# Four narrow modulation products per tile instead of two wide ones, issued together on TensorE

## The chip, the cores and the metric

The kernel runs on one core of one Trainium2 chip. The metric is the device time of one execution in microseconds (us), the median of several runs.

## What is computed

The reference chains two small diffusion-transformer parts over 256 tokens of 1024 features, in float32. Every sublayer is modulated by a condition vector `c`: the vector goes through SiLU and is multiplied by a matrix of modulation weights, which gives rows of 1024 values for shift, scale and gate. Cut to what matters here:

```python
cond = silu(c)                                   # 1 x 1024
for i in range(2):                               # first block: two layers
    shift, scale, gate = split(cond @ ada_w[i] + ada_b[i], 3)
    h = rms_norm(x, norm_g[i]) * (1 + scale) + shift
    x = x + gate * mixer(h)                      # attention with its projections
c_act = silu(c_2)                                # second block
shift1, scale1, gate1, shift2, scale2, gate2 = split(c_act @ w_ada + b_ada, 6)
h = rms_norm(x, norm1_g) * (1 + scale1) + shift1
x = x + gate1 * (attention(h) @ w_out)
h2 = rms_norm(x, norm2_g) * (1 + scale2) + shift2
x = x + gate2 * peer(h2)                         # routing to 16384 small experts
out = rms_norm(x, final_g)
```

The twelve rows of 1024 modulation values are computed as six groups `g` of 2048 columns, each the product of a 1024-long condition and a 1024 x 2048 matrix.

## The kernel before, in words

The program runs through layer 0 (to about 280 us), layer 1 (to about 410 us), the second block's attention (to about 560 us) and the expert stage (to the end). Most matrix products are made from split operands: a float32 tile is split into a high part (ScalarE, line 186) and the rest (VectorE, line 211), and three matmuls (lines 239 to 241) are summed for each product. Weights come in tiles of 512 KB through SyncE's queue (SP): `load_raw` at line 229 for projections, lines 362 and 390 for modulation.

A modulation group is computed by `ada(g)`. The condition, one column for each slice `k` of 128 features, is repeated to 32 columns and is the stationary operand (128 x 32), so a product fills 32 of TensorE's 128 columns, one of four column groups; `tile_position=(0, 32 * q)` names the group. For each of eight slices `k` and each half `h` of the 2048 columns, line 390 loads a tile `adaw` of 128 x 1024 values, and lines 391 to 394 multiply it as two products of 512 columns: half 0 goes to column groups 0 and 1, half 1 to groups 2 and 3. All add up in one PSUM tile `psa` of 128 x 512, whose partitions 32q to 32q + 31 hold the 512 values of quarter `q`. There are 16 tiles and 32 products in a group. Three buffers `adaw` are shared by all tiles. After the last product, line 400 adds the bias row, and for shift and scale `ada_cols` (line 406) turns rows into columns. Operands are float32 without a split; a product then shows in the trace as two weight loads and two matmul records.

Group 0 is needed first and has a function of its own, `ada_first` (line 365), before 50 us. Groups 1 to 5 are the steps `a1` to `a5` in the hand-written order of each layer. There `@-4` shifts a step by four times 50 places to the front:

```python
ORDER = {'0': '... s010 z0 a1@-4 q1 ... v01@-4 s100 a2@-4 z2 ... o O a3@-1',
 '1': ...
 '2': '... sa1 oa1 vb tb sb0@5 a4 ob0@1 sb1 a5 o ob1 O@5'}
```

The order of the steps gives priorities only. When the program is built, a planner with a model of the durations walks through it and puts each engine's instructions into a fixed order: of those whose operands are there by its model, the one with the first priority. At run time every engine and the SP queue keep that order, and wait at an instruction whose operands are late. So the planner places the products of a tile wherever TensorE has a place by its model; the products of one tile need not stand together.

Other lines that the prediction names: 517 (the transposed and normalised input), 631 (transposes of queries and keys), 701 and 706 (transposes of probabilities and their product with the values), 725 and 1117 (attention scores), 820 (the compression product of layer 0: float32 products of 256 columns in two column groups of 64), 898 (transpose of compressed probabilities), 985 (gate logits), 1206 (values of the second block).

Of the kernel before, what the change touches and what calls it, by code (L numbers as in the profile page):

```python
# [21 lines left out]
NK = 8  # L22
# [84 lines left out]
def _consts():  # L107
    c = np.zeros((128, _CW), np.float32)
    p = np.arange(128)

    def put(name, v):
        o, w = _CST[name]
        c[:, o:o + w] = v

    put("ident", np.eye(128))
    put("mask2", np.concatenate([np.zeros((128, 128)), np.where(p[None] > p[:, None], NEG, 0.0)], 1))
    cm = np.full((128, 2, 16), NEG)
    for tt in range(2):
        for n in range(15):
            cm[:, tt, n] = np.where(16 * n + 31 <= tt * 128 + p, 0.0, NEG)  # L120
    put("cmask", cm.reshape(128, 32))
    put("rowok", np.stack([p >= 31, p >= -1], 1))
    put("rmask", p[:, None] // 32 == np.arange(4)[None])
    sel = np.zeros((128, 2, 64))
    for par in range(2):
        sel[2 * np.arange(64) + par, par, np.arange(64)] = 1
    put("sel", sel.reshape(128, 128))
    put("sel4", p[:, None] == 32 * np.arange(4)[None])
    sr = np.zeros((128, 4, 128))
    for j in range(4):  # L130
        sr[32 * j, j, :] = 1
    put("selrow", sr.reshape(128, 512))
    put("iota", np.broadcast_to(p[None], (128, 128)))
    inv = np.array([0x3f800000, 0x3e4693af, 0x3d1a08c8, 0x3beef74e, 0x3ab95d22, 0x398fc8f8,
                    0x385f10c4, 0x372d07a7], np.uint32).view(np.float32)
    put("invf", np.broadcast_to(inv[None], (128, 8)))
    cc = np.arange(64)
    st = np.clip(cc - 8, 0, 48)
    win = (cc[None] >= st[:, None]) & (cc[None] < st[:, None] + 16)
    put("namask", np.tile(np.where(win, 0.0, NEG), (2, 1)))  # L140
    put("ones", 1.0)
    t5 = np.zeros((128, 1024), np.float32)
    for i in range(512):
        rel = min(i - 255, 255)
        t5[_bucket(rel), i] = 1.0
        t5[:, 512 + i] = 0.0 if abs(rel) <= 128 else NEG
    return c, t5


class Net:  # L150
# [230 lines left out]

    def ada(self, g):

        nc, a = self.nc, self.a
        ci = 0 if g < 3 else 8
        ps = self.pp.tile([128, 512], F32, name="psa", tag="psa", bufs=1)
        for k in range(NK):
            for h in range(2):
                raw = self.cp.tile([128, 1024], F32, name="adaw", tag="adaw", bufs=CFG["adaw"])
                nc.sync.dma_start(raw, a["adaw"][g, k, :, h * 1024:(h + 1) * 1024])  # L390
                for j in range(2):
                    q = 2 * h + j
                    nc.tensor.matmul(ps[32 * q:32 * q + 32], self.cond[:, ci + k, :], raw[:, j * 512:(j + 1) * 512],  # L393
                                     start=(k == 0), stop=(k == NK - 1), tile_position=(0, 32 * q))
        gate = g in (1, 4)
        r = self.cp.tile([128, 512], F32, name="adar", tag=f"adar{gate}")
        for q in range(4):
            nc.sync.dma_start(r[32 * q:32 * q + 32], bass.AP(tensor=a["adab"].tensor, offset=(g * 4 + q) * 512,
                                                            ap=[[0, 32], [1, 512]]))
        nc.vector.tensor_tensor(r, ps, r, op=OP.add)  # L400
        if gate:
            self.gr = r
        else:
            self.mods[g] = self.ada_cols(r, ps, (2, 3, 5).index(g) + 1)
# [1189 lines left out]
def _arrays(i):  # L1594
    f = {k: np.ascontiguousarray(np.asarray(v)) for k, v in i.items()}
    o = {}
    o["x"] = f["x"].reshape(S, D)
    cst, t5 = _consts()
    o["cst"], o["t5c"] = cst, t5
    o["cc"] = np.concatenate([f["c"].reshape(8, 128).T, f["c_2"].reshape(8, 128).T], 1)  # L1600
    pos = f["positions"].reshape(S)
    o["pos"] = pos.reshape(2, 128).T
    o["posc"] = np.tile(pos[np.minimum(16 * np.arange(16) + 31, 255)], 4).reshape(64, 1)
    cols = lambda g: g.reshape(8, 128).T
    o["ng"] = np.stack([cols(f["norm_g"][0]), cols(f["norm_g"][1]), cols(f["norm1_g_2"][0]), cols(f["norm2_g_2"][0])], 1)
    o["rows"] = np.concatenate([f["nsa_gate_b"][0], f["nsa_q_norm"][0], f["nsa_k_norm"][0].reshape(-1),
                                f["moba_q_norm"][0], f["moba_k_norm"][0], f["sink_a_2"][0]])
    W, B = f["ada_w"], f["ada_b"]
    W2, B2 = f["w_ada_2"][0], f["b_ada_2"][0]
    split = np.concatenate([np.arange(512) + o for o in (0, 1024, 512, 1536)])  # L1610
    parts = [(W[0][:, split], B[0][split]),
             (np.concatenate([W[0][:, 2048:], W[1][:, 2048:]], 1), np.concatenate([B[0][2048:], B[1][2048:]])),
             (W[1][:, 0:2048], B[1][0:2048]),
             (W2[:, 0:2048], B2[0:2048]),
             (np.concatenate([W2[:, 2048:3072], W2[:, 5120:6144]], 1), np.concatenate([B2[2048:3072], B2[5120:6144]])),
             (W2[:, 3072:5120], B2[3072:5120])]
    o["adaw"] = np.stack([p[0].reshape(8, 128, 2048) for p in parts])
    o["adab"] = np.stack([p[1].reshape(4, 512) for p in parts])

    kt = lambda w, n=512: w.reshape(4, 2, 128, -1, n).transpose(3, 0, 2, 1, 4).reshape(-1, 4, 128, 2 * n)  # L1620

    zt = lambda w: w.reshape(2, 4, 128, -1, 256).transpose(3, 0, 2, 1, 4).reshape(-1, 2, 128, 1024)
    zp = np.concatenate([np.concatenate([np.arange(64) + 64 * (4 * (2 * p + a) + r) for a in range(2)])
                         for p in range(2) for r in range(4)])
    w = f["nsa_w_in"][0]
    o["w0"] = kt(np.concatenate([w[:, 1024:1536], w[:, 1536:1792], w[:, 2048:2304], w[:, 1792:2048], w[:, 2304:2560],
                                 w[:, 0:1024]], 1))
    g = np.zeros((1024, 128), np.float32)
    g[:, :48] = w[:, 2560:2608]
    o["w0g"] = g.reshape(8, 128, 128).transpose(1, 0, 2).reshape(128, 1024)  # L1630
    o["gb"] = f["nsa_gate_b"][0].reshape(48, 1)
    o["w0z"] = zt(w[:, 2608:3632][:, zp])
    o["w0o"] = kt(f["nsa_w_out"][0][zp])
    o["pe"] = f["nsa_cmp_pe"][0].reshape(2, 16, 128).transpose(2, 0, 1)
    o["cw1"] = f["nsa_cmp_w1"][0].reshape(2, 4, 4, 128, 256).transpose(0, 1, 3, 2, 4).reshape(2, 4, 128, 1024)
    o["cb1"] = f["nsa_cmp_b1"][0]
    o["cw2"] = f["nsa_cmp_w2"][0].reshape(2, 2, 128, 64).transpose(2, 0, 1, 3)
    w = f["moba_w_in"][0]
    o["w1"] = kt(np.concatenate([w[:, 1024:1536], w[:, 0:1024]], 1))
    o["w1z"] = zt(w[:, 1536:2560][:, zp])  # L1640
    o["w1o"] = kt(f["moba_w_out"][0][zp])
    w = f["w_in_2"][0]
    o["w2s"] = kt(w[:, 512:768], 256)[0]
    o["w2"] = kt(np.concatenate([w[:, 0:512], w[:, 768:2304]], 1))
    za = np.concatenate([np.concatenate([np.arange(64) + 64 * (4 * a + r) for a in range(2)]) for r in range(4)])
    w = f["w_out_2"][0]
    o["w2o"] = kt(np.concatenate([w[0:512][za], w[512:]], 0))
    o["on"] = np.concatenate([f["out_norm_a_2"][0][za].reshape(4, 128).T, f["out_norm_b_2"][0].reshape(4, 128).T], 1)
    o["t5t"] = f["t5_table_2"]
    o["rpb"] = f["rpb_b_2"].reshape(8, 15, 31)  # L1650
    o["wq"] = zt(f["w_query_2"][0])
    o["keys"] = f["sub_keys_2"][0].reshape(16, 128, 128).transpose(2, 0, 1)
    o["u"] = f["u_experts_2"][0].reshape(128, 128, 8, 128).transpose(0, 3, 2, 1).reshape(128, 128, 1024)
    o["v"] = f["v_experts_2"][0].reshape(128, 128, 1024)
    o["fg"] = f["final_g_2"]
    return {k: np.ascontiguousarray(v) for k, v in o.items()}
# [16 lines left out]
```

## Time and profile before

| | us |
|---|---|
| median of 3 runs | 1414.01 (1412.24 to 1414.22) |
| the profiled execution | 1413.74 |
| its span in the trace | 1412.0 |
| TensorE busy in the span | 1366.8 (97%) |
| VectorE busy | 1023.2 (72%) |
| ScalarE busy | 821.9 (58%) |
| matmuls of line 393, busy | 81.3 |

Times in the trace count from the start of the span. A row of the timeline is a run of like records of an engine, with its start, its length and the number of records; the end of a matmul is modelled and reaches into the next one, so a cost is read from one start to the next start. A float32 product of line 393 or 820 has two records. In the windows, "busy" is the union of an engine's records in that stretch and the number in brackets counts them. "PEld" is TensorE's loading of the stationary operand. In the list of waits, "SPq" is the queue in which SyncE issues the loads.

### The profile page before, as it was taken

Reading aid. Unit: us, or ns where it says so; the run is one execution under the profiler, and the core shown is the slowest. Engines: PE = TensorE matmul, PEld = TensorE weight load, DVE = VectorE, ACT = ScalarE, POOL = GpSimd, SP = SyncE. Lnnn points to the kernel's source line nnn. Section 1 sums busy time; section 2 is a strip of 40 time slices with the busy share of each in tenths; the row PEclk is TensorE's granted clock in tenths of the full one; section 3 lists DMA queues with packets and bytes.
Section 4 is the critical chain, followed back from the end, with each engine's and each line's share of the span. In section 5 each row is a group of like instructions: output and inputs, shape, how many; then the busy total and the mean of one; then the engine's idle time right before and its main releaser. Section 6 shows DMA issues by size and latency. Waiting matters only on the chain.

```text
span 1412.0 us, 24444 instructions
## 1 busy us (share of the span) xinstructions
PE 1366.8 (97%) x8522; PEld 1120.8 (79%) x8522; DVE 1023.2 (72%) x2636; ACT 821.9 (58%) x1887; POOL 21.9 (2%) x27
## 2 busy tenths in 40 slices
PE   6999999999989998999999999999999999999997
PEld 2566666477767755999999999999998888888885
DVE  3585756388665656799999968888866666677777
ACT  2353656357646654555555568888865555555554
POOL 0000000000001100000000000000000000000001
PEclk9999999999999999999999999999999999999999
DMA  8577564553486766455555555554456665677773
GB/s 309 199 272 273 197 203 138 199 186 101 138 313 199 216 225 223 135 182 179 179 179 179 181 188 193 165 164 162 165 194 227 194 194 194 194 227 239 245 242 114
DMA packets 94875, 279.15 MB, mean 198 GB/s; under 512 B 11112, under 2 KB 30320, under 8 KB 94624
## 3 DMA queue, kind: packets, MB, share of 16 engines
q1 hardware_dynamic: 94752, 277.59, 59.6%
q8 instruction: 67, 1.10, 0.3%
q14 instruction: 56, 0.46, 0.1%
HBM read 267.80 MB, written 13.94 MB: 200 GB/s over the span
## 4 chain that ended last, share of the span: by engine, by line
PE 90%; DVE 4%; DMA 4%; ACT 1%; issue 1%; SPq 0%; ACTq 0%; DVEq 0%
PE ps L240 18%; PE ps L239 18%; PE ps L241 18%; PE acc L240 5%; PE acc L239 5%; PE acc L241 5%; PE psa L393 5%; PE ps L1493 4%; PE ps L706 2%; DMA raw<-in_w1o 1%; PE ps L725 1%; PE ps L701 1%; PE psa L365 1%; DMA adaw<-in_adaw 1%; DVE lo L211 1%; PE ps L631 1%
## 5 line engine op out<-in xcount | busy, mean ns | idle before, releaser
L186 ACT CAST hi<-raw 128x512 fp32r<-128x512 f32 (+1 forms) x700 | 429.4, 618 | 349.9 <-PE ps L240 147.1
L211 DVE TENSOR_TENSOR lo<-raw,hi 128x512 fp32r<-128x512 f32 (+1 forms) x700 | 479.8, 688 | 179.7 <-ACT hi L186 162.8
L239 PE MATMUL ps<-hh,hi 128*128 128x256 f32 x1160 | 333.0, 287 | 1.3 <-DVE hh L187 1.3
L240 PE MATMUL ps<-hl,hi 128*128 128x256 f32 x1160 | 328.3, 283 | 1.1 <-DVE hl L211 1.1
L241 PE MATMUL ps<-hh,lo 128*128 128x256 f32 x1160 | 328.4, 283 | 0.0
L239 PEld LDWEIGHTS ps<-hh,hi 128*128 128x128 f32 x1160 | 222.6, 192 | 1.5 <-issue 1.5
L240 PEld LDWEIGHTS ps<-hl,hi 128*128 128x128 f32 x1160 | 222.4, 192 | 1.3 <-DVE hl L211 1.3
L241 PEld LDWEIGHTS ps<-hh,lo 128*128 128x128 f32 x1160 | 222.2, 192 | 0.0
L239 PE MATMUL ps<-hi,Ah 128*128 128x512 f32 x508 | 198.1, 390 | 0.0
L240 PE MATMUL ps<-lo,Ah 128*128 128x512 f32 x508 | 197.7, 389 | 0.0
L241 PE MATMUL ps<-hi,Al 128*128 128x512 f32 x508 | 197.6, 389 | 0.0
L239 PEld LDWEIGHTS ps<-hi,Ah 128*128 128x128 f32 x508 | 95.4, 188 | 20.1 <-issue 0.2
L241 PEld LDWEIGHTS ps<-hi,Al 128*128 128x128 f32 x508 | 95.4, 188 | 19.9
L240 PEld LDWEIGHTS ps<-lo,Ah 128*128 128x128 f32 x508 | 95.4, 188 | 19.9 <-DVE lo L211 0.2
L1492 ACT ACTIVATE og<-o,gT 128x128 f32<-128x128 bf16 x256 | 87.2, 394 | 4.1 <-DVE o L1490 0.3
L393 PE MATMUL psa<-adaw,cond 128*32 128x512 f32 x320 | 81.3, 610 | 3.1 <-DMA adaw<-in_adaw 3.1
L240 PE MATMUL acc<-lo,hh 128*128 128x512 f32 (+1 forms) x176 | 70.7, 402 | 2.4 <-DVE lo L211 2.4
L239 PE MATMUL acc<-hi,hh 128*128 128x512 f32 (+1 forms) x176 | 69.6, 401 | 2.6 <-DVE hh L187 1.4
L241 PE MATMUL acc<-hi,hl 128*128 128x512 f32 (+1 forms) x176 | 69.9, 398 | 0.0
L1493 PE MATMUL ps<-og,o 128*128 128x128 f32 x512 | 65.2, 275 | 0.1
L1493 PEld LDWEIGHTS ps<-og,o 128*128 128x128 f32 x512 | 61.4, 192 | 0.3 <-ACT og L1492 0.3
L733 ACT ACTIVATE P<-P,nm 128x128 f32<-128x128 f32 (+1 forms) x96 | 42.6, 446 | 13.5 <-DVE nm L730 13.4
(397 smaller groups left out, 1929.8 us busy)
## 6 DMA issues: line engine op xcount, KB each, us to landing
raw<-in_u SPq DMA_DIRECT2D x128, 512.0 KB, 3.6
raw<-in_v SPq DMA_DIRECT2D x128, 512.0 KB, 4.3
adaw<-in_adaw SPq DMA_DIRECT2D x86, 512.0 KB, 4.9
raw<-in_w SPq DMA_DIRECT2D x48, 512.0 KB, 4.3
raw<-in_wq SPq DMA_DIRECT2D x16, 512.0 KB, 3.4
zd<-ge SPq DMA_DIRECT2D x56, 128.0 KB, 1.7
ge<-zd SPq DMA_DIRECT2D x56, 128.0 KB, 3.6
raw<-in_adaw SPq DMA_DIRECT2D x10, 512.0 KB, 7.0
```

The lines of the kernel that those rows point to most:

```text
L186: return self.nc.scalar.copy(out, in_)
L211: return self.nc.vector.tensor_tensor(lo, src, hi.bitcast(F32), op=OP.subtract)
L239: mm(out, a[0][asl], b[0][bsl], start=first, stop=False, **kw)
L240: mm(out, a[0][asl], b[1][bsl], start=False, stop=False, **kw)
L241: mm(out, a[1][asl], b[0][bsl], start=False, stop=last, **kw)
L365: nc.tensor.matmul(ps[32 * q:32 * q + 32], self.cond[:, k, :], raw[:, j * 512:(j + 1) * 512], start=(k == 0), stop=(k == NK - 1), tile_pos ...
L393: nc.tensor.matmul(ps[32 * q:32 * q + 32], self.cond[:, ci + k, :], raw[:, j * 512:(j + 1) * 512], start=(k == 0), stop=(k == NK - 1), til ...
L631: nc.tensor.transpose(pr[:P, i * 128:i * 128 + 128], s.rearrange("p a d -> p (a d)") if P == 128 else s, self.identr)
L706: nc.tensor.matmul(o[64 * a:64 * a + 64], v[br][kb][:, 2 * pair + a, :], pts[a], start=first, stop=False, tile_position=(0, 64 * a), skip_ ...
L733: nc.scalar.activation(Pb, Pb, AF.Exp, scale=-1.0, bias=nm[:, r, br:br + 1], accum_out=sums[:, r, br:br + 1])
L1492: nc.scalar.activation(og[:, j], o1[:, j], AF.Copy, scale=gT[:, t0 + j:t0 + j + 1])
L1493: nc.tensor.matmul(ps[:, j * 128:j * 128 + 128], o2[:, j], og[:, j], start=(j == 0), stop=(j == 3), skip_group_check=True)
```

## The change

A tile `adaw` now holds 256 columns of each of the four quarters. It is multiplied as four products of 256 columns, one for each column group; half `h` fills columns 256h to 256h + 255 of `psa`. The three products after the first get a priority that is 2000 places ahead, and an edge for the planner that puts them behind the first. The start flag stands at the first half of the first slice alone, the stop flag at the second half of the last. The array `adaw` is rearranged to fit for groups 1 to 5; group 0 and `ada_first` stay as they were.

```diff
@@ def ada(self, g)
             for h in range(2):
                 raw = self.cp.tile([128, 1024], F32, name="adaw", tag="adaw", bufs=CFG["adaw"])
                 nc.sync.dma_start(raw, a["adaw"][g, k, :, h * 1024:(h + 1) * 1024])
-                for j in range(2):
-                    q = 2 * h + j
-                    nc.tensor.matmul(ps[32 * q:32 * q + 32], self.cond[:, ci + k, :], raw[:, j * 512:(j + 1) * 512],
-                                     start=(k == 0), stop=(k == NK - 1), tile_position=(0, 32 * q))
+                first = None
+                for q in range(4):
+
+                    with self.tc.high_priority(offset=2000) if first else ExitStack():
+                        i = nc.tensor.matmul(ps[32 * q:32 * q + 32, h * 256:h * 256 + 256], self.cond[:, ci + k, :],
+                                             raw[:, q * 256:q * 256 + 256], start=(k == 0 and h == 0),
+                                             stop=(k == NK - 1 and h == 1), tile_position=(0, 32 * q), skip_group_check=True)
+                    if first:
+                        self.tc.add_manual_dep(i.ins, first.ins.name, mybir.DependencyInfo(
+                            mybir.DependencyClass.NoSync, mybir.DependencyReason.DATA), reason="order of issue")
+                    first = first or i
@@ def _arrays(i)
-    o["adaw"] = np.stack([p[0].reshape(8, 128, 2048) for p in parts])
+    o["adaw"] = np.stack([p[0].reshape(8, 128, 2048) if g == 0 else
+                          p[0].reshape(8, 128, 4, 2, 256).transpose(0, 1, 3, 2, 4).reshape(8, 128, 2048)
+                          for g, p in enumerate(parts)])
```

## Rows read from the trace of the kernel before

**Rows 1.** The page, busy time, share of the span and instructions of each engine

```profile
PE 1366.8 (97%) x8522; PEld 1120.8 (79%) x8522; DVE 1023.2 (72%) x2636; ACT 821.9 (58%) x1887; POOL 21.9 (2%) x27
```

**Rows 2.** Windows: length, busy time (records) by engine, granted clock, DMA share, GB/s

```profile
400.00:547.00 147.00, 143.09 (x781) 92.76 (x781) 91.11 (x235) 91.01 (x215) 14.13 (x17) 1.00 0.74 239
81.00:547.00 466.00, 453.70 (x2573) 299.65 (x2571) 302.63 (x984) 264.23 (x658) 16.02 (x19) 1.00 0.61 205
```

**Rows 3.** The same windows, instructions of line 393 alone

```profile
81.00:280.00 199.00, 46.88 (x180) 7.00 (x180) 0.99 0.61 209
400.00:547.00 147.00, 29.12 (x116) 4.13 (x116) 1.00 0.74 239
81.00:547.00 466.00, 81.16 (x320) 11.94 (x320) 1.00 0.61 205
```

**Rows 4.** Chain of waits from 81 to 547 us, its shares by line

```profile
by line: PE psa L393 14.4%; PE acc L239 13.5%; PE acc L240 13.5%; PE acc L241 13.3%; PE ps L706 5.3%; DMA raw<-in_w1o 4.2%; PE ps L725 4.0%; PE ps L701 3.6%; PE ps L631 2.5%; DMA adaw<-in_adaw 2.2%; DVE lo L211 2.1%; PE ps L1117 1.8%; DMA r
```

**Rows 5.** TensorE's timeline: start, us, line, tiles, records, [idle before <- releaser]

```profile
134.25 1.07 PE L393 MATMUL psa<-adaw,cond 128*32 128x512 f32 x8
135.24 0.50 PE L725 MATMUL ps<-kT,qT 128*128 128x256 f32 x2
135.68 1.04 PE L393 MATMUL psa<-adaw,cond 128*32 128x512 f32 x2
136.65 0.38 PE L239 MATMUL acc<-hh,hi 128*128 128x256 f32 x1
```

**Rows 6.** TensorE's timeline around 83.8 us

```profile
83.27 0.40 PE L240 MATMUL acc<-lo,hh 128*128 128x512 f32 x1
83.51 0.39 PE L241 MATMUL acc<-hi,hl 128*128 128x512 f32 x1
83.83 1.90 PE L393 MATMUL psa<-adaw,cond 128*32 128x512 f32 x10
85.66 0.50 PE L239 MATMUL acc<-hi,hh 128*128 128x512 f32 x1
```

**Rows 7.** TensorE's timeline, first and last of 70 stretches of line 393

```profile
81.50 1.04 PE L393 MATMUL psa<-adaw,cond 128*32 128x512 f32 x2
...
546.09 1.05 PE L393 MATMUL psa<-adaw,cond 128*32 128x512 f32 x4 [0.62 <-DMA adaw<-in_adaw]
```

**Rows 8.** TensorE's timeline, line 820 and what follows

```profile
108.91 3.73 PE L820 MATMUL ps<-raw,kcr 128*64 128x256 f32 x30
112.58 1.90 PE L393 MATMUL psa<-adaw,cond 128*32 128x512 f32 x10
```

**Rows 9.** Window of 0.1 us, line 393: matmuls and weight loads begun

```profile
83.80:83.90 0.10, 0.07 (x4) 0.07 (x8) 1.00 0.17 62
```

**Rows 10.** TensorE's timeline, stretches of line 393 that wait

```profile
101.91 1.45 PE L393 MATMUL psa<-adaw,cond 128*32 128x512 f32 x8
...
238.61 1.91 PE L393 MATMUL psa<-adaw,cond 128*32 128x512 f32 x12
241.71 0.30 PE L898 MATMUL ps<-ident,cmpP 128*128 128x128 f32 x1 [1.19 <-DVE cmpP L895]
...
243.68 1.92 PE L393 MATMUL psa<-adaw,cond 128*32 128x512 f32 x4 [1.13 <-DMA adaw<-in_adaw]
...
410.16 1.07 PE L393 MATMUL psa<-adaw,cond 128*32 128x512 f32 x8
412.60 1.05 PE L393 MATMUL psa<-adaw,cond 128*32 128x512 f32 x4 [1.38 <-DMA adaw<-in_adaw]
```

**Rows 11.** Waits of SP's queue, 81 to 547 us: total, times, longest

```profile
SPq L390 <- PE psa L393: 113.9, 42, 8.2
SPq L229 <- DVE lo L211: 100.3, 35, 9.3
```

**Rows 12.** Window of 400 to 440 us, columns as in rows 2

```profile
400.00:440.00 40.00, 36.72 (x209) 29.15 (x209) 31.79 (x77) 25.09 (x56) 2.23 (x1) 1.00 0.85 293
```

**Rows 13.** Window of 243.3 to 246.7 us, columns as in rows 2

```profile
243.30:246.70 3.40, 3.02 (x9) 1.02 (x10) 0.00 (x0) 0.05 (x2) 0.00 (x0) 0.51 0.62 222
```

## The prediction

> **What bounds the kernel now.** I read the page's head first: TensorE is busy for 97% of the span, VectorE for 72% [rows 1]. A share over the whole span can hide stages, so next I cut out the stretch in which the changed products run. All 320 of their matmul records lie between 81 and 547 us (each product has two records, because a product of float32 operands goes through TensorE as two passes over its columns). There TensorE is busy for 453.7 of 466 us, VectorE for 302.6 and ScalarE for 264.2; the 16 DMA engines have a mean share of 0.61 [rows 2]. So TensorE sets the pace in this stretch, with 12.3 us of idle time in all. The modulation products of line 393 take 81.2 us of it: 46.9 up to 280 us, in layer 0, and 29.1 from 400 us, for the most part in the second block [rows 3]. In the chain of waits over the same stretch line 393 has 14.4%, which is 67 of 466 us [rows 4]. Less time in this line is therefore less time on the path, until something else is late.
>
> **What one product costs, and what two or four cost together.** The timeline of TensorE around 134 us has the key reading [rows 5]. A lone product (2 records) starts at 135.68 and the next operation starts at 136.65: 0.97 us. Four products (8 records) start at 134.25 and the next operation starts at 135.24: 0.99 us. Four products that write four column groups cost what one costs; each further one adds about 7 ns. Five products cannot do that, since only four column groups exist: 83.83 to 85.66, 1.83 us [rows 6]. So a further round on busy groups costs 1.83 - 0.97 = 0.86 us, two passes of 0.43 us for 512 columns, and 0.97 - 0.86 = 0.11 us is what entering the small tiles and leaving them adds behind the start. Before the start another 0.08 us is lost: the matmul ahead of 83.83 started at 83.51, 0.32 us earlier, where that one and its neighbour are 0.24 us apart [rows 6].
>
> I followed all stretches of line 393 in that timeline. There are 70, from the first at 81.50 to the last at 546.09 [rows 7]: 26 with one product, 23 with two, 6 with three, 8 with four, 7 with five or six. Without the waits inside, they cost 26 x 0.98 + 23 x 0.98 + 6 x 0.99 + 8 x 1.00 + 7 x 1.84 = 74.8 us. Seven in ten stretches use one or two of four column groups.
>
> **The change, part by part.** A tile (512 KB, 1024 columns) is now multiplied as four products of 256 columns, one for each column group, instead of two of 512. The nearest rows for 256 float32 columns in column groups are those of line 820, which uses two groups: 30 records in 108.91 to 112.58 [rows 8]. That is 15 pairs of passes in 3.67 us, and less the 0.11 and 0.08 us of the switch 0.23 us for a pass with its own start. Half of 0.43 is 0.215 us, which I take; at 0.23 all tiles together would cost 80 x 2 x 0.015 = 2.4 us more.
> - A tile that follows another tile costs two passes, 0.43 us. A tile alone costs 0.43 + 0.11 + 3 x 0.007 = 0.57 us, and 0.08 us more ahead of it.
> - Bounds: all 80 tiles alone, 80 x 0.57 = 45.6 us, with ten more entries than the 70 of before, 0.8 us: 46.4. If about 60 stretches are left because some tiles meet, as they do now where a stretch has three or more products: 80 x 0.43 + 60 x 0.13 - 0.8 = 41.4 us. I take 43, between them, nearer the lower end: 21 stretches of now hold three or more products, so tiles do meet. TensorE's gain is 74.8 - 43 = **31.8 us**.
> - The products double from 160 to 320 and so do the weight loads. Eight of these loads began within 0.1 us, with four matmuls already under way [rows 9], so they lie beside the passes. If that cover were gone, each of 320 added loads at 0.11 us would be 35 us; the last rival takes that up.
> - The order of columns in the source array, the start and stop flags and the unchecked groups: nothing on the device. The loads stay 80 of 512 KB, in the same rows, and the addition at line 400 has the same shape.
> - The order: the three products behind a tile's first are put next in line. Nothing else is queued past on SP or POOL by hand. But urgent matmuls now wait behind 0.57 us at most for a tile, not 0.97 for one of its halves; a gain too small to count.
>
> **What will be late next.** Three kinds of wait eat into the gain.
> - Stretches that wait for their own tiles. At 238.61 six products last until 241.71 and at 243.68 two take 1.92 us instead of about 1.05, with an operand or a load as the last to come [rows 10]. Seven stretches, from the one at 101.91 to the one at 410.16, with 31 of the 160 products, are longer than the pattern in this way. A faster product there only waits longer: 31/160 of 31.8 us is 6 us that I strike off. This is an estimate; between none of it and twice as much.
> - Operands in the second block. 29.1 of the 81.2 us lie there [rows 3], between softmax heads and their transposes, with the DMA share at 0.74 [rows 2]. Its part of the gain is 11.4 us; I take half, 5.7 us, as lost to VectorE, ScalarE and loads (ends: none, and all).
> - The loads themselves. SP waited 42 times for line 393 to release a tile buffer, 113.9 us, but 35 times for VectorE's split of the weights (100.3 us) [rows 11]. Of 80 tile loads 42 move up with the products; the others stand in SP's queue behind weight loads. This says that the two deductions are not the whole story, and makes the lower end: 42/80 of 31.8 is 17 us, less the 6 us of the first point, 11 us.
>
> Sum: 31.8 - 6 - 5.7 = 20.1 us. The profiled execution took 1413.74 us, its span 1412.0 and 1.7 us around it; it becomes 1393.6. The median of the three runs, 1414.01, is 0.3 us above it, so I say **1394 us**. After 547 us nothing changes, and the shift should stay constant to the end. A measurement of this kernel can tell 0.2%, 2.8 us, from no change.
>
> **The rivals.**
> - *Waits take most of it* (0.17). If the planner, which orders the instructions ahead of time, puts operands no earlier, TensorE idles where line 393 was a filler. For it: idle time of only 12.3 us means that the fillers cover something now. Against it: VectorE and ScalarE are busy for under two thirds of the stretch [rows 2]. Gain 5 to 11 us, say 1406.
> - *All of it arrives, or more* (0.13). If the other engines keep up, 31.8 us come through: 1382.
> - *Slower: tile loads jump the queue* (0.06). A buffer is free as soon as its four products are issued together, so the planner may place a tile load in SP's queue ahead of a weight load that the path waits for. Place: 400 to 440 us and the end of layer 1, where DMA runs at 293 GB/s and a load of 512 KB therefore takes 1.8 us of all engines [rows 12]. From 11 such loads on the path (20 us) it eats the gain; 16 give 29 us and 1423. Against it: the same loads in the same number, and a mean DMA share of 0.61.
> - *The three products do not come next, or the groups do not overlap* (0.02). A product alone of 256 columns is 0.97 - 0.43 = 0.54 us; 320 of them are 173 us, 98 us more than now: 1512. Against it: the four starts of [rows 9]. The remaining 0.62 is the forecast with its own range, 1386 to 1402.
>
> A rule speaks for the last rival. In the trace, eight weight loads began in the 0.1 us in which four matmuls were under way, all on the same 128 rows [rows 9]. The Trainium skill, TensorE: Matmul & The Clock Gate, section Part 3: Packing small matmuls, says that a weight load overlaps matmuls in flight only when its row group differs. By that rule the products of a tile, which differ in column group alone, would go one after the other with their loads between, and the sum would be that rival's or worse. The trace disagrees, so it gets no more than the 0.02.
>
> One smaller cost is in the range: TensorE's granted clock was 0.51, the 1.2 GHz level, from 243.3 to 246.7 us, after 1.19 and 1.13 us of idle time [rows 10, 13]. More idle stretches may bring a few more of these. One costs at most half of its 3.4 us, 1.7 us; three are 5 us.
>
> **The numbers.** Forecast 0.62, rivals 0.17, 0.13, 0.06, 0.02. The range runs from 1381 to 1408: it takes in the forecast, the full gain, and most of the case in which waits take the gain, and leaves out the slower rivals, the tail of the waits and a planner's luckier order, under 0.2 together. Faster 0.90 (forecast, full gain and nearly all of the waits), same 0.03 (the rest of the waits), slower 0.07.
>
> **What would show it.** In the new timeline, stretches of 8 records that start within 0.03 us, second passes 0.24 us later, 0.57 us to the next operation; line 393's successor at some 40 to 47 us of TensorE time; the stage after 560 us about 20 us earlier, with more than half of it won before 300 us. Wrong, if tiles cost 0.9 us or more; if idle time of TensorE between 81 and 547 us grows from 12 to over 30 us; or if the shift at 560 us is not that of the end.

## The result and the profile after

| | before | changed |
|---|---|---|
| median, us | 1413.96 (1412.24 to 1414.22, 4 runs) | 1391.71 (1389.95 to 1394.32, 4 runs) |
| profiled execution, us | 1413.74 | 1390.83 |
| its span, us | 1412.0 | 1389.1 |

The ratio is 0.9843, with a 95% interval of 0.9825 to 0.9861: 22 us faster. In a later run (`after_again`) the same kernel gave 1392.57 against 1416.74, a ratio of 0.982 (0.979 to 0.985).

Lines have moved in the changed kernel: 390 is now 391, 393 is 396, and 517, 631, 701, 706, 725, 820, 1117 are 525, 639, 709, 714, 733, 828, 1125. Its page's busy times, which answer to [rows 1]:

```profile
PE 1339.5 (96%) x8842; PEld 1126.9 (81%) x8842; DVE 1023.2 (74%) x2636; ACT 820.2 (59%) x1887; POOL 21.8 (2%) x27
```

And rows of its TensorE timeline, which answer to [rows 5]:

```profile
105.93 1.07 PE L396 MATMUL psa<-adaw,cond 128*32 128x256 f32 x16
106.93 0.50 PE L828 MATMUL ps<-raw,kcr 128*64 128x256 f32 x2
...
132.44 0.64 PE L396 MATMUL psa<-adaw,cond 128*32 128x256 f32 x8
133.00 0.51 PE L733 MATMUL ps<-kT,qT 128*128 128x256 f32 x2
```

From start to next start, a lone tile (8 records) takes 0.56 us and two tiles together 1.00 us; 0.57 and 0.57 + 0.43 were forecast. TensorE's busy time falls by 27 us over the kernel; VectorE's does not move, and ScalarE's hardly.

Where the time came from is read from windows by stage. The bounds are the starts of the next stage's transposed input (line 517 or 525). The kernel before, with length, busy time (records) of PE, PEld, DVE, ACT, POOL, granted clock, DMA share, GB/s:

```profile
80.00:283.40 203.40, 197.41 (x1146) 121.08 (x1144) 124.92 (x455) 103.17 (x272) 0.95 (x1) 0.99 0.61 210
283.40:414.50 131.10, 125.42 (x699) 93.34 (x699) 100.81 (x334) 79.57 (x195) 3.17 (x2) 1.00 0.49 170
414.50:564.00 149.50, 143.63 (x796) 95.33 (x796) 92.05 (x241) 89.52 (x209) 11.90 (x16) 0.99 0.71 226
80.00:564.00 484.00, 466.45 (x2640) 309.75 (x2638) 317.78 (x1028) 272.25 (x676) 16.02 (x19) 0.99 0.61 204
```

The changed kernel, the same stages:

```profile
80.00:266.00 186.00, 179.04 (x1346) 122.57 (x1345) 122.98 (x454) 101.47 (x269) 0.95 (x1) 0.99 0.66 230
266.00:398.70 132.70, 124.63 (x726) 94.45 (x727) 100.56 (x334) 79.75 (x196) 3.17 (x2) 0.99 0.50 172
398.70:540.30 141.60, 134.41 (x885) 97.53 (x885) 92.98 (x242) 89.01 (x209) 11.81 (x16) 0.98 0.72 232
80.00:540.30 460.30, 438.08 (x2957) 314.56 (x2955) 316.52 (x1028) 270.22 (x674) 15.93 (x19) 0.99 0.63 214
```

The modulation products alone over the whole of it, before (line 393), where the columns are PE, PEld, clock, DMA share and GB/s:

```profile
80.00:564.00 484.00, 81.30 (x320) 11.94 (x320) 0.99 0.61 204
```

And changed (line 396):

```profile
80.00:540.30 460.30, 48.50 (x640) 13.97 (x640) 0.99 0.63 214
```

Layer 0 is 17.4 us shorter, layer 1 is 1.6 us longer, the second block is 7.9 us shorter. Over the three, the modulation takes 32.8 us less of TensorE (81.3 to 48.5). All other work on it takes 4.4 us more (466.45 - 81.30 = 385.2, and 438.08 - 48.50 = 389.6), and its idle time grows by 4.7 us, from 17.6 to 22.2. That gives 32.8 - 4.4 - 4.7 = 23.7 us, which is the shift from 564.0 to 540.3. The later stage keeps nearly all of it: 22.9 us at the end of the span.

The chain of waits of the changed kernel begins only at 229.90 us, so its shares over this stretch do not compare with [rows 4]. From the start of layer 1 to the end of the second block both chains are whole: there line 396 has 4.9% of 274 us, 13 us, where line 393 had 9.1% of 281 us, 26 us. The line below is the head of the changed kernel's chain, with shares of the stretch from 80 us on.

```profile
by line: PE acc L241 10.0%; PE acc L240 9.9%; PE acc L239 9.7%; DMA raw<-in_w1o 4.3%; PE psa L396 4.1%; PE ps L714 3.3%; DVE lo L211 2.1%; PE ps L709 2.0%; PE ps L525 2.0%; PE ps L1125 1.8%; PE ps L639 1.7%; PE ps L733 1.3%; DMA adaw<-in_ad
```

### The profile page after: what moved, and what is told of

Read it like the earlier page. It is cut to its first block, busy times and chain, and to the rows that moved or that the text cites. A ratio compares the mean times of both kernels' runs of the same rounds, so it can differ in the third digit from the quotient of the medians.

```text
span 1389.1 us, 25082 instructions
## 1 busy us (share of the span) xinstructions
PE 1339.5 (96%) x8842; PEld 1126.9 (81%) x8842; DVE 1023.2 (74%) x2636; ACT 820.2 (59%) x1887; POOL 21.8 (2%) x27
## 4 chain that ended last, share of the span: by engine, by line
PE 77%; DVE 3%; DMA 2%; ACT 1%; issue 0%; ACTq 0%; DVEq 0%
PE ps L241 18%; PE ps L240 18%; PE ps L239 18%; PE ps L1501 4%; PE acc L241 3%; PE acc L240 3%; PE acc L239 3%; DMA raw<-in_w1o 1%; PE psa L396 1%; PE ps L714 1%; PE ps L525 1%; DVE lo L211 1%; PE ps L709 1%; PE ps L1125 1%; PE ps L639 1%; PE ps L1398 1%
## 5 line engine op out<-in xcount | busy, mean ns | idle before, releaser
L396 PE MATMUL psa<-adaw,cond 128*32 128x256 f32 x640 | 48.5, 390 | 4.7 <-DMA adaw<-in_adaw 4.3
L1498 DVE TENSOR_TENSOR o<-iof,eT 128x512 bf16<-128x512 f32 x64 | 44.2, 691 | 8.2 <-ACT og L1500 7.5
```

Source lines behind the costliest of these rows:

```text
L396: i = nc.tensor.matmul(ps[32 * q:32 * q + 32, h * 256:h * 256 + 256], self.cond[:, ci + k, :], raw[:, q * 256:q * 256 + 256], start=(k == ...
L1498: v.tensor_tensor(o1, iob, eT[0][:, t0:t0 + 4, None].to_broadcast([128, 4, 128]), op=OP.is_equal)
```

## Experiments

All runs in one table. Below the kernel before, they are ordered by the time that the modulation products keep TensorE busy between 80 us and the end of the second block, where the expert stage's transposed input starts. "Other work" is TensorE's remaining busy time there, "idle" what is left of the stretch. The last four columns are of one profiled execution each. Medians and ratios are of 4 runs (10 for `e2_order_only` and `e3_two_groups`) against the kernel before on the same chip. Its median there was 1415.81 for `e1_layout_only`, `e2_order_only`, `e3_two_groups` and `e8_twice`, 1416.74 for `after_again`, `e4_narrow`, `e5_eight` and `e6_four_buffers`, and 1414.17 for `e7_adaw2`, `e9_offset100`, `e10_half_width` and `e11_fillers`. Every edit also gives the planner something else to order, so the other work differs a little between runs. Line 396 is 395 in `e2_order_only`; in `e4_narrow` and `e10_half_width` the lines from 394 on are one higher.

| run | median, us | ratio (95%) | modulation | other work | idle | stretch |
|---|---|---|---|---|---|---|
| before | 1413.96 | | 81.3 | 385.2 | 17.6 | 484.0 |
| e8_twice | 1435.43 | 1.0157 (1.0128 to 1.0186) | 82.7 | 394.5 | 27.0 | 504.2 |
| e3_two_groups | 1407.32 | 0.9948 (0.9926 to 0.997) | 69.0 | 386.5 | 20.8 | 476.3 |
| e2_order_only | 1410.0 | 0.9965 (0.9947 to 0.9982) | 68.7 | 388.9 | 19.1 | 476.7 |
| e1_layout_only | 1404.39 | 0.9924 (0.9896 to 0.9953) | 63.5 | 391.0 | 21.1 | 475.6 |
| e9_offset100 | 1400.22 | 0.9901 (0.9881 to 0.9921) | 56.6 | 389.5 | 23.4 | 469.5 |
| e7_adaw2 | 1402.33 | 0.9906 (0.9887 to 0.9925) | 50.8 | 397.2 | 29.5 | 477.4 |
| changed | 1391.71 | 0.9843 (0.9825 to 0.9861) | 48.5 | 389.6 | 22.2 | 460.3 |
| after_again | 1392.57 | 0.982 (0.979 to 0.985) | 48.2 | 389.8 | 24.2 | 462.2 |
| e11_fillers | 1395.4 | 0.9871 (0.9845 to 0.9896) | 47.6 | 389.1 | 24.1 | 460.8 |
| e5_eight | 1398.97 | 0.9878 (0.9851 to 0.9905) | 47.0 | 392.6 | 28.9 | 468.4 |
| e6_four_buffers | 1392.41 | 0.9827 (0.9796 to 0.9859) | 45.5 | 390.6 | 25.6 | 461.7 |
| e10_half_width | 1387.98 | 0.9812 (0.9793 to 0.9831) | 32.7 | 393.2 | 29.0 | 454.9 |
| e4_narrow | 1386.96 | 0.9785 (0.9758 to 0.9813) | 22.1 | 402.3 | 33.6 | 457.9 |

### The parts of the change, one at a time

**e1_layout_only**: the new layout, order left to the planner.

```diff
-                    with self.tc.high_priority(offset=2000) if first else ExitStack():
+                    with ExitStack():
...
-                    if first:
-                        self.tc.add_manual_dep(...)
```

> The new layout (four products of 256 columns for a tile) without the high priority and the edge behind the first product: the planner may put the four anywhere, and now does in 86 stretches, 26 of them with one product. Theory (the gain is TensorE time, and it comes where four column groups run together): by 0.57 us for a stretch of up to four products and 0.43 us for each further round, line 394 costs some 13 us more than in the changed kernel; at the ratio seen, 22.9 us of span for 31.3 us of TensorE time, that is 10 us: about 1401. Rival (the narrow layout alone does it): 1392. Rival (the order alone does it): 1414.

Measured: 1404.39, with 15 us more of modulation time than changed (63.5 and 48.5). About half of the gain is there without any rule of order: in many places the planner puts several products of a tile together by itself, and only 26 of the 86 stretches hold one product.

**e2_order_only**: the old layout, the second product next in line (an edit of the kernel before).

```diff
+                first = None
                 for j in range(2):
                     q = 2 * h + j
-                    nc.tensor.matmul(ps[32 * q:32 * q + 32], ...)
+                    with self.tc.high_priority(offset=2000) if first else ExitStack():
+                        i = nc.tensor.matmul(ps[32 * q:32 * q + 32], ...)
+                    if first:
+                        self.tc.add_manual_dep(i.ins, first.ins.name, ...)
+                    first = first or i
```

> The old layout (two products of 512 columns for a tile, two column groups), with the second product put next in line behind the first. Theory (TensorE time): no stretch of one product is left, 63 stretches in place of 70, at 0.98 us each and 0.86 for a further round, 12 us less TensorE time than before; at 22.9 / 31.3 that is 9 us: about 1405. Rival (the order alone brings the whole gain): 1392. Rival (only the layout counts): 1414.

Measured: 1410.0. The modulation time fell by 12.6 us as expected; the span gave 5 to 6 us of it, not 9. A quarter of the change's gain, so neither the order alone nor nothing.

**e3_two_groups**: four products of 256 columns, next in line, on two column groups (an edit of the kernel before).

```diff
...
+                for c in range(2):
                     for j in range(2):
                         q = 2 * h + j
...
+                            i = nc.tensor.matmul(ps[32 * q:32 * q + 32, c * 256:c * 256 + 256], self.cond[:, ci + k, :],
+                                                 raw[:, j * 512 + c * 256:j * 512 + c * 256 + 256], ...)
...
```

> The old layout of a tile on two column groups, but as four products of 256 columns, all put next in line: products as many and as narrow as in the changed kernel, only two column groups at a time. Theory (four groups together make the gain): a tile costs 4 passes of 0.215 us and 0.12 us, 0.98 us, so some 7 us less than before and 24 us more than changed: about 1408. Rival (narrow products next in line are enough): 1392.

Measured: 1407.32, as the theory had it. The rows of its timeline stand against those at 132.44 us above: the same eight records of 128x256, 0.98 us on two column groups and 0.56 us on four.

```profile
133.62 1.06 PE L396 MATMUL psa<-adaw,cond 128*32 128x256 f32 x8
134.60 0.39 PE L239 MATMUL acc<-hh,hi 128*128 128x256 f32 x1
```

So neither narrow products nor their order make the whole gain by themselves. Four column groups at a time make it, and the order rule brings the four together where the planner alone does not.

**e9_offset100**: `high_priority(offset=100)` in place of 2000.

> The changed kernel with the three products put 100 places ahead instead of 2000: the planner now splits some tiles again, 80 stretches, 12 of them with one product, some 7 to 8 us more TensorE time in line 396 than in the changed kernel. Theory (TensorE time of the products): 5 to 7 us slower than changed, 1397 to 1400. Rival (any priority is enough, the order does it): within 3 us of changed.

Measured: 1400.22. A weaker rule leaves the planner room to split tiles, 8 us of modulation time come back, and about as much of the span.

**e8_twice**: each product issued twice, so that the sums are doubled.

```diff
...
-                for q in range(4):
+                for q in (0, 1, 2, 3, 0, 1, 2, 3):
...
```

> The changed kernel with every product of line 396 issued twice, so the modulation sums are doubled: 0.43 us more for each of 80 tiles, 34.6 us of TensorE time put back at the same places. Theory (span follows this TensorE time, at 0.73 to 1.0): 25 to 35 us more than changed, 1417 to 1427. Rival (the gain came from another order of the rest, not from the time of the products): 1392 to 1398.

Measured: 1435.43, some 43 us more than the changed kernel, beyond the theory's range and far from the rival's. The products give 34.2 us of it (82.7 and 48.5), where they should; 4.9 us are other work and 4.8 us idle time that the theory had not. The idle time comes with longer waits of the products for their own tile loads: 10.5 us, where the changed kernel has 4.3.

```profile
PE psa L396 <- DMA adaw<-in_adaw: 10.5, 13, 1.7
```

The window of its whole stretch:

```profile
80.00:584.20 504.20, 477.20 (x3585) 334.74 (x3578) 319.01 (x1022) 271.23 (x674) 16.05 (x19) 0.99 0.60 195
```

And its modulation products alone:

```profile
80.00:584.20 504.20, 82.73 (x1272) 34.18 (x1264) 0.99 0.60 195
```

It has about the modulation time of the kernel before and is 20 us slower. So the span does not follow the products' time alone. The planner also sees twice the products and orders everything else anew; where the other work comes from stays open.

### What takes the rest of the gain

**e4_narrow** and **e10_half_width**: the products of slices 1 to 7 keep 32 or 128 of their 256 columns. The diff is that of e4_narrow; the other has 128 for 32.

```diff
+                n = 32 if k else 256
...
-                        i = nc.tensor.matmul(ps[32 * q:32 * q + 32, h * 256:h * 256 + 256], self.cond[:, ci + k, :],
-                                             raw[:, q * 256:q * 256 + 256], ...)
+                        i = nc.tensor.matmul(ps[32 * q:32 * q + 32, h * 256:h * 256 + n], self.cond[:, ci + k, :],
+                                             raw[:, q * 256:q * 256 + n], ...)
```

> The changed kernel with the products of slices 1 to 7 cut to their first 32 columns (7/8 of those columns are left out); loads, order rules and number of products stay. Line 397 loses some 28 us more of TensorE time. Theory A (TensorE still bounds the stretch; the gain of this change was cut only by small waits): at the ratio of this change, 0.73, 20 us less than changed: 1371. Theory B (loads and operands of other engines are late next, so the gain runs out): less than half of it arrives, 1380 to 1390, and TensorE's idle time between 80 us and the end of the second block grows from 22 to over 35 us.

> As e4_narrow, but the products of slices 1 to 7 keep 128 of their 256 columns: some 15 us less TensorE time in line 397 than changed. If the gain runs out as in e4_narrow (28 us less gave 6), 2 to 6 us faster than changed, 1387 to 1391, with more idle time and more time at the lower clock than changed (12 us between 80 us and the end of the second block) and less than e4_narrow (42 us). If TensorE time still counted at 0.7: 1382.

Measured: 1386.96 and 1387.98. Twenty-six us less of modulation time than changed bring 5 to 6 us against `after_again` on the same chip, sixteen bring 1 to 4 by the ratios; the intervals of both overlap with those of the changed kernel. So the change has taken most of what there is to take: of a further cut of the products little reaches the span. In e4_narrow other work rises to 402.3 us, by 12.7, and the clock gives nearly all of it. By the record of the granted clock, TensorE is busy with other work for 34 us of the stretch at the 1.2 GHz level, where the changed kernel has 9.7 us; half of the difference, 12 us, is an estimate of what that costs. Its window of 120 to 160 us:

```profile
120.00:160.00 40.00, 35.86 (x244) 31.22 (x240) 28.15 (x105) 21.43 (x60) 0.00 (x0) 0.87 0.65 223
```

And TensorE's timeline in it:

```profile
119.86 0.27 PE L397 MATMUL psa<-adaw,cond 128*32 128x32 f32 x8
120.90 0.44 PE L837 MATMUL ps<-ident,hid 128*128 128x128 f32 x2 [0.77 <-ACT hid L834]
124.08 0.58 PE L239 MATMUL acc<-hh,hi 128*128 128x256 f32 x1 [2.74 <-ACT hi L186]
...
126.02 0.42 PE L240 MATMUL acc<-hl,hi 128*128 128x256 f32 x1
126.23 0.41 PE L241 MATMUL acc<-hh,lo 128*128 128x256 f32 x1
...
130.85 0.28 PE L240 MATMUL acc<-hl,hi 128*128 128x256 f32 x1
130.97 0.28 PE L241 MATMUL acc<-hh,lo 128*128 128x256 f32 x1
```

After two waits of TensorE, 0.77 and 2.74 us, equal matmuls stand 0.21 us apart (126.02 to 126.23) until about 130 us and 0.12 us apart later (130.85 to 130.97): first 1.2 GHz, then 2.4. In the changed kernel the same window has a granted clock of 1.00; over the stretch of 457.9 us e4_narrow has 0.95. The Trainium skill, TensorE: Matmul & The Clock Gate, section HAM oscillation, says that waits between groups of matmuls bring the clock down, so that the next group starts slowly; this trace agrees. Not every wait does it: after the 2.11 us before 385.11 in the changed kernel the granted clock stays at 1.00. The expectation for e10_half_width was wrong in one point: its time at the lower clock, 12.5 us by the granted clock's record, is about that of the changed kernel (12.0), and its loss is idle time (29.0 us).

**e5_eight**: both tiles of a slice as one chain of eight products.

```diff
-                first = None
+                first = first if h else None
```

> Both tiles of a slice as one chain: the eight products of tiles h = 0 and h = 1 are put next in line behind the first. The planner now joins 15 pairs. Theory (a stretch costs 0.2 us for going in and out of the small tiles): some 3 us less TensorE time, 1389 to 1392. Rival (the second tile's load is waited for at the head of the queue): 1394 or more, with more idle time before line 396.

Measured: 1398.97, 6 us slower than `after_again`. The rival's time was right: TensorE saves 1.5 us of products, but idles 6.7 us more than the changed kernel and has 3.0 us more of other work. Waits of line 396 for its loads, which the rival named, are 3.0 us of the idle time; the rest is spread over other waits. Its list of TensorE's waits (total, times, longest) has the loads of tiles:

```profile
PE psa L396 <- DMA adaw<-in_adaw: 7.3, 9, 1.6
```

The same wait in the changed kernel:

```profile
PE psa L396 <- DMA adaw<-in_adaw: 4.3, 4, 2.4
```

**e6_four_buffers** and **e7_adaw2**: `adaw` 4 instead of 3 (with `pt0` 3 for 5 and `f2k2` 2 for 3, to make room), and 2 instead of 3.

> The changed kernel with four tile buffers instead of three; their space comes from two other rings (pt of layer 0 from 5 to 3, f2k of the second block from 3 to 2). Theory (part of the lost gain are products that wait for their own loads, 4 to 8 us): 4 to 7 us faster than changed, 1385 to 1388, and the waits of line 396 for its loads shrink. Rival (the loads come late because SP's queue stands at other waits, not for want of buffers): within 3 us of changed, or slower by what the two smaller rings cost.

> The changed kernel with two tile buffers instead of three. Since four buffers gave nothing, one theory is that SP's order of other waits holds the loads back, so that two buffers cost little: 1392 to 1397. The other is that three buffers are just enough and two bind: every tile then waits for a load of about 5 us, some 15 us slower or more, 1405 and up.

Measured: 1392.41 and 1402.33. With a fourth buffer nothing changes that can be told (waits of line 396 for its loads are even 7.9 us), so a lack of buffers is probably not what holds the loads back; what the two smaller rings cost was not measured alone. But two buffers cost 10 us, between the two theories. In the waits of SP's queue, the wait of a tile load for an earlier tile load grows from 17.5 to 57.9 us, while the wait for VectorE's split of the weights, an operand and not a tile buffer, stays. SP's queue in e7_adaw2:

```profile
SPq L229 <- DVE lo L211: 113.8, 40, 11.1
SPq L391 <- PE psa L396: 97.0, 60, 7.0
SPq L391 <- DMA adaw<-in_adaw: 57.9, 34, 5.7
```

SP's queue in the changed kernel, which answers to [rows 11]:

```profile
SPq L229 <- DVE lo L211: 118.1, 37, 14.2
SPq L391 <- PE psa L396: 90.9, 50, 6.3
SPq L391 <- DMA adaw<-in_adaw: 17.5, 18, 3.3
```

**e11_fillers**: steps a1 and a2 without `@-4`.

> The changed kernel with steps a1 and a2 at their own places instead of 200 places ahead, so that in layer 0 their products fill waits of TensorE rather than stand ahead of other work. Theory (the rest of the gain is lost where TensorE idles and its clock falls, and products placed there cost nothing): less idle time up to the end of layer 0 than the 7 us of changed, and 2 to 5 us faster, 1388 to 1391. Rival (the modulation is then late for its users): slower than changed, 1395 or more, with idle time at line 435 or in the gates.

Measured: 1395.4, from 1390.36 to 1399.5. No gain, and the ratios' intervals overlap. Idle time in its layer 0 is 8.9 us, against 7.0. That the modulation came late for its users is not shown either. Of the kernels that do the whole computation none is measurably faster than the changed one.

## Why the prediction was right, step by step

1394 us was forecast and 1391.71 measured, inside 1381 to 1408 and inside the likeliest case's own range.

- **Price of a tile**: right. 0.56 us alone, 1.00 for two. The weight loads lie beside the passes, as [rows 9] had it: in the changed kernel, too, eight loads and four matmuls begin within 0.1 us, and 0.3 us after the start all eight passes are under way. Two windows of line 396, as in [rows 9]:

```profile
132.40:132.50 0.10, 0.06 (x4) 0.07 (x8) 1.00 0.61 82
132.60:132.70 0.10, 0.10 (x8) 0.00 (x0) 1.00 0.00 0
```

  Had the last rival been right, they would stand one after the other; e3_two_groups, where each group's passes do queue, shows what queueing looks like.
- **Number of stretches**: 65 (55 of one tile, five of two, five of three), where 60 to 80 were the bounds and 43 us the sum; without waits inside they cost 55 x 0.57 + 5 x 1.00 + 5 x 1.43 = 43.5 us, so the gain on TensorE was 31.3 us, not 31.8. (The 48.5 us of the window, a little above the 40 to 47 forecast, are busy time with modelled ends that reach into the next record.)
- **Deductions**: 11.7 us were struck off, all for waits, and 8.4 are missing (31.3 and 22.9). The size was near, the places were not; that the sum came this close is partly luck. TensorE's idle time grew by 4.7 us only, and about 4 us were lost to the clock (below), which the sum had at nothing. One long stretch was misread as well: the two products at 243.68 took 1.92 us because they ran at the 1.2 GHz level [rows 13], not for a wait inside. Layer 0 gave all of its gain (17.4 of 17.8 us), although the long stretches at 101.91 and 238.61 [rows 10] were counted as lost there. Layer 1, which had no term of its own, gave nothing: its modulation saved 2.6 us, and the stage became 1.6 us longer. Here the rule of the long stretches did hold. Three tiles, in place of five products, take 381.50 to 385.11, 3.61 us with an operand's wait at the end. The changed kernel's timeline:

```profile
381.50 1.50 PE L396 MATMUL psa<-adaw,cond 128*32 128x256 f32 x24
385.11 0.50 PE L239 MATMUL acc<-hi,ozh 128*128 128x512 f32 x1 [2.11 <-ACT hi L186]
```

  Before, five products took 3.54 us at the same place:

```profile
397.33 1.90 PE L393 MATMUL psa<-adaw,cond 128*32 128x512 f32 x10
400.87 0.51 PE L239 MATMUL acc<-hi,ozh 128*128 128x512 f32 x1 [1.64 <-ACT hi L186]
```

  The operand comes from a load of `in_w1o` that is on the chain in both kernels, 19.4 us long before, until 400.10, and 19.6 us in the changed kernel, until 384.34; the split of the operand follows it. Shorter products under it only lengthen the wait, from 1.64 to 2.11 us. Before:

```profile
380.69 19.41 DMA raw<-in_w1o
```

  Changed:

```profile
364.75 19.59 DMA raw<-in_w1o
```

  The second block lost about a third (7.9 us of some 12), where half was struck off.
- **The clock**: foreseen as a smaller cost, "a few more of these", and found, at about the size that the prediction gave for three. Layer 1 begins with one: after an idle stretch of 1.87 us that ended at 270.81, the granted clock is 0.50 from 272.3 to 275.7 us, with matmuls 0.43 us apart (272.81 to 273.23) that stand 0.24 us apart just before. In three such windows TensorE is busy for 9.9 us at the lower level, all but 0.2 with other work; the kernel before had one, 3.0 us, of which 1.9 were products of line 393. Half of the difference in other work (9.7 and 1.1) is some 4 us, so by this estimate the clock makes nearly all of the 4.4 us by which other work grew. The three windows:

```profile
115.30:118.70 3.40, 3.18 (x16) 2.06 (x18) 0.00 (x0) 0.00 (x0) 0.00 (x0) 0.50 0.86 348
272.30:275.70 3.40, 3.40 (x12) 2.19 (x15) 3.14 (x8) 1.14 (x2) 0.00 (x0) 0.50 0.41 155
398.60:402.00 3.40, 3.29 (x15) 3.32 (x16) 0.69 (x4) 1.21 (x4) 0.00 (x0) 0.50 1.07 355
```

And the timeline around the start of the second:

```profile
271.88 0.40 PE L239 MATMUL acc<-hi,hh 128*128 128x512 f32 x1
272.12 0.47 PE L240 MATMUL acc<-lo,hh 128*128 128x512 f32 x1
...
272.81 0.63 PE L239 MATMUL acc<-hi,hh 128*128 128x512 f32 x1
273.23 0.63 PE L240 MATMUL acc<-lo,hh 128*128 128x512 f32 x1
```

- **The rivals**: the full gain did not come, and e4_narrow shows that even 26 us less of products bring only 5 to 6 more. Waits and the clock together took about a quarter of the gain, not most. That tile loads jump SP's queue was not seen in the changed kernel's time; no run tried it alone. (The chances of the two slower rivals add up to 0.08, where the prediction says 0.07.)

## What to carry to other kernels

Look at what one, two and four products cost together before asking how many there are: where the second to fourth are nearly free, a layout that gives each column group its share of every tile gets the gain from the tile itself instead of from luck. An order rule has to be strong enough to hold against the planner, but chaining what waits for a second load gives part of the gain back (6 us here). On an engine at 97% a saving arrived at about three quarters here, until the next waits were bare; then idle time and a lower clock ate most of a further cut.

## What the runs showed that was not expected

With the modulation products cut to an eighth of the columns (e4_narrow), layer 0 takes 192 us (80 us to 272.2) in place of 186, although its products take 14 us less there: TensorE's idle time grows from 7.0 to 18.1 us and its other work from 149.8 to 159.1 us, with a mean granted clock of 0.87 in the 40 us from 120 us on. So products that fill waits can also keep the neighbours' clock up. At half of the columns (e10_half_width) the time at the lower clock did not grow, and the planner's order differs too, so how much filling it takes is not shown. And a second pass on top of the same tiles (e8_twice) costs more than its own time, 43 us for 34.
